# A recurrent scan of two directions with its per-head products laid on the two diagonal quarters of the matrix array, and with new ranks for its steps

## Chip, cores and metric

One core of one Trainium2 chip runs the whole program. The metric is the device time of one execution in microseconds (us). The kernel before takes 3224.84 us, the median of 3 runs (3218.99 to 3229.81).

## What is computed

The program is one block of a network on 1024 tokens of width 1024 and 256 context tokens. A projection feeds three parts: windowed attention (8 heads of 64), a recurrent scan (8 heads of 64) that runs over the tokens in both directions, and gates. Their results are merged, and a layer of 16 experts follows. The change concerns the scan. For each head it keeps a 64x64 state S and does, at each token:

```python
sa = jnp.einsum('bhvk,bhk->bhv', S, -kk_t)
S = (S * w_t[:, :, None, :] + sa[..., None] * (kk_t * a_t)[:, :, None, :]
     + v_t[..., None] * k_t[:, :, None, :])
y = jnp.einsum('bhvk,bhk->bhv', S, r_t) if emit else None
```

Each direction first goes over the 256 context tokens, of which no y is kept, and then over the 1024 tokens.

## The kernel before, in words

The tokens go in chunks of 64, so a direction has 20 steps: 4 for the context and 16 main ones. What a chunk needs is made ahead of the scan, in the feature stage (`feat`, one call for each of four column tiles `ct` of 128 features, that is, of two heads): the matrices X (from kk and r), AQ and BT (products within a chunk, masked or transposed) and WT (the inverse of a triangular 64x64 matrix, made on VectorE by `inv` and `inv_off`). They are written to DRAM (XD, AQD, BTD, WD; the values to vD), and each step of the scan loads its chunk from there.

The feature stage's inner loop, `jb` over 5 blocks of 4 chunks, runs 40 times in all (4 tiles, 2 directions). In each pass it makes X, copies AQ out of PSUM (L427), masks it (L429), writes it with three small DMAs (L430, L432; L433 in the context's block), transposes BK, copies BT out of PSUM on ScalarE (L440, a single buffer) and writes it to BTD with one DMA (L441). All these DMAs are issued by SP.

The scan is `rwkv_chain`, 20 steps for each of two directions, the directions in turn. A step of the kernel before does this:

- It loads its matrices with six or seven DMAs on SP (L527 to L534). AQ and UV hold two things one above the other: partitions 0 to 63 are for U (zeroed by GpSimd at L529 where it is not yet known), partitions 64 to 127 hold the values V.
- L538: X times the state S, four products with 128 rows, 128 columns and 128 moving columns. S holds the two heads of a tile as a block diagonal, half of it zeros.
- L541: AQ times UV for the eight heads, added to the same PSUM tile RY; 128 rows, 64 output columns, always the same output half (partitions 0 to 63).
- L545 and L546: RY is copied to R, negated; the even heads by ScalarE, the odd ones by VectorE to the upper partitions.
- L550: WT times R, eight products of 64x64x64, the even head on partitions 0 to 63 and the odd one on 64 to 127, in rows and in output.
- L553: the result U is copied into UV, the even heads by VectorE and the odd ones by ScalarE.
- L556: BT times UV, 128 rows, the output half alternating with the head.
- L561 and L562: the state gets the sum added and is scaled by the decay; VectorE, two instructions each, one for each half.
- In a main step, L565: AQ's second half times UV, all on output partitions 64 to 127; L568 copies y out of PSUM and L569 stores it, from ScalarE's queue.

A planner orders each engine's instructions when the program is built: it simulates the run and, of the instructions that are ready, takes the one with the lowest rank. A rank is the place in the order of the program; `low_priority(tc, n)` adds n to the ranks inside it. At run time each engine goes through its list in that order. The scan stands in the program ahead of the last seven of 16 gate projections (`proj` with `on_gate`, L258 and L265), ahead of the attention of tiles 0 and 1 (`att((0,1),...)`), the readout and the attention of tiles 2 and 3. Attention's tiles first load and rotate q and k (L627 to L643), then go through eight blocks each (`block`, L588 to L617). The scan's PSUM tiles, two for each direction, and those of attention 0 and 1 fill the eight banks; the readout and attention 2 and 3 take their banks over.

## Time and profile before

| | |
|---|---|
| median of 3 runs | 3224.84 us (3218.99 to 3229.81) |
| the profiled execution's own time | 3227.2 us |
| its span | 3225.4 us |
| TensorE (PE) busy | 2975.9 us, 92% |
| VectorE (DVE) busy | 2361.4 us, 73% |
| ScalarE (ACT) busy | 1742.2 us, 54% |
| GpSimd (POOL) busy | 639.5 us, 20% |
| mean granted clock of TensorE | 0.953 |

Rows are read as follows. PE is the stream of matrix products and PEld that of their weight loads; SPq and ACTq are queues that issue DMAs. A group of instructions has its line, engine, operation, tiles (out<-in), shape and count, then busy time and mean duration, then the engine's idle time just before its members and what ended it. A 32-bit product counts as two instructions on PE, so eight products show as x16. Products overlap in the array, so the spacing of a run of them is read from its whole length less the length of one, divided by one less than their count.

### The profile page before, as it was taken

How to read it: one execution, taken by the hardware profiler on the slowest of the kernel's cores; microseconds unless marked ns; L12 is line 12 of the kernel's file. 1: busy time of each engine (PE TensorE's matmuls, PEld its weight loads, DVE VectorE, ACT ScalarE, POOL GpSimd, SP SyncE). 2: the span in 40 equal slices, each digit the busy share in tenths (PEclk: the TensorE clock that was granted, in tenths of full speed). 3: DMA queues.
4: the chain of work that ended last, by engine and by line, in shares of the span. 5: the costliest groups of instructions: out<-in, count | busy, mean ns of one | idle time of the engine just before them, and what ended most of it. 6: DMA issues, size and time to landing. Idle time of an engine off the chain costs nothing.

```text
span 3225.4 us, 47429 instructions
## 1 busy us (share of the span) xinstructions
PE 2975.9 (92%) x17900; PEld 2366.1 (73%) x17900; DVE 2361.4 (73%) x3207; ACT 1742.2 (54%) x2006; POOL 639.5 (20%) x511
## 2 busy tenths in 40 slices
PE   7999999997878978899879999999999999999995
PEld 4777776776667764477668888888888878888884
DVE  5245455544376769757788999888898888888887
ACT  5343343433234334322357777777777777777775
POOL 2233333333241227211000000111010111010004
PEclk8998999998889999899889999999999999999998
DMA  5245554555778766444589999999999999999985
GB/s 205 82 121 137 124 128 123 129 142 131 158 185 203 189 166 219 146 152 151 198 315 384 388 372 370 357 363 377 380 362 363 358 365 376 381 362 362 363 319 229
DMA packets 537641, 825.18 MB, mean 256 GB/s; under 512 B 206590, under 2 KB 335742, under 8 KB 537284
## 3 DMA queue, kind: packets, MB, share of 16 engines
q1 hardware_dynamic: 490876, 747.60, 67.5%
q10 hardware_dynamic: 41176, 55.01, 5.4%
q0 software_dynamic: 5360, 19.54, 2.3%
q8 instruction: 141, 2.31, 0.3%
q14 instruction: 88, 0.72, 0.1%
HBM read 732.49 MB, written 89.55 MB: 255 GB/s over the span
## 4 chain that ended last, share of the span: by engine, by line
PE 45%; DVE 8%; issue 4%; DMA 3%; ACT 2%; POOL 1%; ACTq 0%; POOLq 0%; DVEq 0%; SPq 0%
PE ph L1016 22%; PE ye L1031 14%; DVE lo L915 4%; PE po L752 3%; PE pA L709 2%; PE pt L1053 1%; DMA raw<-in_w_e_dram 1%; ACT hi L914 1%; DVE oh L856 0%; DVE dl L1055 0%; PE pl L828 0%; PE apt L606 0%; PE yp L613 0%; DVE s L599 0%; DMA wmod<-in_w_mod_dram 0%
## 5 line engine op out<-in xcount | busy, mean ns | idle before, releaser
L915 DVE TENSOR_TENSOR lo<-raw,hi 128x2048 fp32r<-128x2048 f32 (+1 forms) x560 | 1197.5, 2170 | 107.9 <-ACT hi L914 92.0
L914 ACT CAST hi<-raw 128x2048 fp32r<-128x2048 f32 (+1 forms) x560 | 1009.8, 1813 | 353.7 <-PE ph L1016 191.0
L1016 PE MATMUL ph<-lo,xh 128*128 128x512 f32 (+1 forms) x1536 | 456.7, 378 | 23.4 <-DVE lo L915 23.1
L1016 PE MATMUL ph<-hi,xh 128*128 128x512 f32 (+1 forms) x1536 | 448.9, 374 | 3.1 <-ACT xh L886 2.0
L1016 PE MATMUL ph<-hi,xl 128*128 128x512 f32 (+1 forms) x1536 | 448.2, 373 | 0.0
L1016 PEld LDWEIGHTS ph<-lo,xh 128*128 128x128 f32 x1536 | 267.6, 188 | 95.4 <-DVE lo L915 48.3
L1016 PEld LDWEIGHTS ph<-hi,xh 128*128 128x128 f32 x1536 | 271.5, 188 | 55.9 <-ACT xh L886 2.4
L1016 PEld LDWEIGHTS ph<-hi,xl 128*128 128x128 f32 x1536 | 270.8, 188 | 52.7
L258 PE MATMUL pp<-uh,whi 128*128 128x512 f32 (+1 forms) x832 | 266.2, 392 | 4.8 <-DVE th L334 3.1
L258 PE MATMUL pp<-ul,whi 128*128 128x512 f32 (+1 forms) x832 | 267.4, 392 | 0.0
L258 PE MATMUL pp<-uh,wlo 128*128 128x512 f32 (+1 forms) x832 | 261.8, 387 | 0.5 <-issue 0.3
L864 POOL DMA_INDIRECT gath<-table,idx x16 | 37.9, 2368 | 958.6 <-DVE oh L856 587.7
L1031 PE MATMUL ye<-lo,dh 128*128 128x512 f32 x704 | 222.5, 397 | 1.1 <-DVE lo L915 0.9
L1031 PE MATMUL ye<-hi,dh 128*128 128x512 f32 x704 | 219.7, 393 | 2.5 <-ACT hi L914 1.3
L1031 PE MATMUL ye<-hi,dl 128*128 128x512 f32 x704 | 218.9, 392 | 3.3 <-DVE dl L1055 3.3
L258 PEld LDWEIGHTS pp<-uh,whi 128*128 128x128 f32 x832 | 155.0, 195 | 42.2 <-issue 7.1
L258 PEld LDWEIGHTS pp<-uh,wlo 128*128 128x128 f32 x832 | 156.6, 196 | 38.2 <-issue 8.8
L258 PEld LDWEIGHTS pp<-ul,whi 128*128 128x128 f32 x832 | 156.3, 196 | 37.5 <-issue 10.0
L292 DVE TENSOR_TENSOR tmp<-AU,W 120x144 f32<-120x144 f32 (+24 forms) x248 | 93.0, 375 | 115.8 <-DMA WD<-AU 40.0
L1031 PEld LDWEIGHTS ye<-hi,dl 128*128 128x128 f32 x704 | 132.8, 189 | 32.1 <-DVE dl L1055 3.7
L207 POOL TENSOR_TENSOR wlo<-wraw,whi 128x512 fp32r<-128x512 f32 x86 | 113.6, 1341 | 211.4 <-ACT whi L206 141.0
L1031 PEld LDWEIGHTS ye<-hi,dh 128*128 128x128 f32 x704 | 131.1, 189 | 30.7 <-ACT hi L914 2.0
(334 smaller groups left out, 4488.8 us busy)
## 6 DMA issues: line engine op xcount, KB each, us to landing
raw<-in_w_e_dram SPq DMA_DIRECT2D x430, 1024.0 KB
raw<-in_w_e_dram SPq DMA_DIRECT2D x128, 768.0 KB
wraw<-in_w_in_dram SPq DMA_DIRECT2D x86, 256.0 KB
wmod<-in_w_mod_dram SPq DMA_DIRECT2D x48, 256.0 KB
BTD<-BT SPq DMA_DIRECT2D x40, 256.0 KB
cBT<-BTD SPq DMA_DIRECT2D x40, 256.0 KB
wmod<-in_w_mod_dram SPq DMA_DIRECT2D x16, 512.0 KB
XD<-X SPq DMA_DIRECT2D x32, 256.0 KB
```

Of the source, the lines that this page charges most:

```text
L207: nc.gpsimd.tensor_sub(l[:,ks],r,h[:,ks].bitcast(F32))
L258: nc.tensor.matmul(p,wt[:,k,:],ut[:,k,a:a+b],start=(k==0 and first),stop=(k==7 and last))
L292: nc.vector.tensor_tensor(v,AU[d][:,:,s,ts_][:,:,None,:].to_broadcast([120,2,nj,L]), W[d][:,:,js,s:s+1].to_broadcast([120,2,nj,L]),op=ALU. ...
L709: nc.tensor.matmul(pq[q],w[:,kk,:],y[:,kk,q*512:(q+1)*512],start=(kk==0 and first),stop=(kk==3 and last))
L752: nc.tensor.matmul(pq[q],a[:,r],w[:,q*512:(q+1)*512],start=(k==0 and first),stop=(k==7 and last))
L864: gi=nc.gpsimd.indirect_dma_start(out=g,out_offset=None,in_=table[:,:], in_offset=bass.IndirectOffsetOnAxis(ap=idx[:,:1],axis=0))
L914: nc.scalar.copy(hi[:,:2*w],r[:,:2*w])
L915: li=nc.vector.tensor_sub(lo[:,:2*w],r[:,:2*w],hi[:,:2*w].bitcast(F32))
L1016: nc.tensor.matmul(PH[m][j][:,:c.stop-c.start],x[:,k,:],y[:,c],start=(k==0 and a),stop=(k==7 and b))
L1031: nc.tensor.matmul(ye[j],l[:,k,:],rr[:,j*512:(j+1)*512],start=st and a,stop=sp and b)
L1053: for k in range(n): nc.tensor.transpose(pt[:,k,:],hd[:,(k0+k)*128:(k0+k+1)*128],ident)
```

## The change

The two heads of a column tile are split by parity: even heads on partitions 0 to 63, odd heads on 64 to 127, for every operand of the scan. Every product becomes 64x64x64 with its rows and its output in the same half (`mm`, eight for a call, the halves in turn; its first two carry the start flag and the rest are ordered behind them). U and V have tiles of their own, so that the combined products with 128 rows become two with 64 each. S loses its zeros. R, U and y are copied by one ScalarE instruction each, over 128 partitions and 256 elements, and the state is updated by two VectorE instructions in place of four. GpSimd's memsets go. In program order the products with V alone are put ahead of those that need R. A main step has 64 products in place of 36, a context step 40 in place of 28. The DRAM tensors get the parity layout: the feature stage writes AVD and AUD in place of AQD, and BTD with four DMAs in place of one; vD and yD get twice the DMAs. On the host, g_up, gn and w_pr are permuted to match. Each pair of steps k = 4j+n gets `low_priority(tc, 2920-96k)`.

```diff
@@ host_layout
+    by=lambda a: np.ascontiguousarray(a.reshape(a.shape[0],4,2,64).transpose(0,2,1,3).reshape(a.shape[0],512))
+    o["g_up"]=by(i["g_up"][0])
...
@@ mixer
+    AVD=[dp.tile([20,128,4,128],F32,name=f"AVD{d}") for d in range(2)]
+    AUD=[dp.tile([20,128,4,64],F32,name=f"AUD{d}") for d in range(2)]
+    BTD=[dp.tile([20,2,128,4,64],F32,name=f"BTD{d}") for d in range(2)]
...
@@ on_v
-                    nc.sync.dma_start(vD[t0*128:(t0+nt)*128,ct*128:(ct+1)*128].rearrange("(a p) f -> p a f",p=128),vt[:,:nt])
+                    for hh in range(2):
+                        nc.sync.dma_start(vD[t0*128:(t0+nt)*128,hh,ct].rearrange("(a p) f -> p a f",p=128),vt[:,:nt,hh*64:hh*64+64])
@@ feat
-                        if jb: nc.sync.dma_start(AQD[d][cs,64:128,2*ct:2*ct+2,:].rearrange("c p h f -> p c h f"),AQ[64:128])
                         for hh in range(2):
-                            if jb: nc.sync.dma_start(AQD[d][cs,0:64,2*ct+hh,64:128].rearrange("c p f -> p c f"),AQ[0:64,:,hh,64:128])
-                            else: nc.sync.dma_start(AQD[d][cs,64:128,2*ct+hh,:w].rearrange("c p f -> p c f"),AQ[64:128,:,hh,:w])
+                            nc.sync.dma_start(AVD[d][cs,hh*64:hh*64+64,ct,:w].rearrange("c p f -> p c f"),AQ[64:128,:,hh,:w])
+                            if jb: nc.sync.dma_start(AUD[d][cs,hh*64:hh*64+64,ct].rearrange("c p f -> p c f"),AQ[0:64,:,hh,64:128])
...
-                        nc.sync.dma_start(BTD[d][cs,:,ct,:].rearrange("c p f -> p c f"),BT)
+                        for j in range(2):
+                            for hh in range(2):
+                                nc.sync.dma_start(BTD[d][cs,j,hh*64:hh*64+64,ct].rearrange("c p f -> p c f"),BT[j*64:j*64+64,:,hh*64:hh*64+64])
@@ rwkv_chain (the lines taken out are those told above)
+    H=[slice(0,64),slice(64,128)]
+    def mm(o,l,r,first=None,stop=False):
+        for ct in range(4):
+            for hh,h in enumerate(H):
+                b=first is not None and len(first)<2
+                z=nc.tensor.matmul(o[h,ct],l[h,ct],r[h,ct],start=b,stop=stop,skip_group_check=True)
+                if b: first.append(z)
+                elif first: tc.add_manual_dep(z.ins,first[hh].ins.name,mybir.DependencyInfo(mybir.DependencyClass.NoSync,mybir.DependencyReason.DATA),reason="order")
...
+        nc.sync.dma_start(AV[:,:,:M],G["AVD"][d][cc][:,:,:M])
+        for h,hh in zip(H,range(2)): nc.sync.dma_start(V[h],vD[cc*64:(cc+1)*64,hh])
         nc.sync.dma_start(X[:,:,:M],G["XD"][d][:,:,cc,:M].rearrange("a p f -> p a f"))
+        for h,hh in zip(H,range(2)):
+            nc.sync.dma_start(WT[h],G["WD"][d][:,cc*2+hh,0:64,:].rearrange("a s t -> s a t"))
+        nc.sync.dma_start(BT,G["BTD"][d][cc].rearrange("j p a k -> p j a k"))
+        if main: nc.sync.dma_start(AU,G["AUD"][d][cc])
+        RU=pR.tile([128,2,4,64],F32,name=f"RU{d}"); YS=pR.tile([128,2,4,64],F32,name=f"YS{d}")
+        mm(RU[:,0],AV[:,:,0:64],V,[],first)
+        if not first: mm(RU[:,0],X[:,:,0:64],S[d],stop=True)
+        R=p.tile([128,4,64],F32,name=f"R{d}",bufs=1)
+        nc.scalar.activation(R,RU[:,0],AF.Copy,scale=-1.0)
+        f=[]
+        mm(YS[:,1],BT[:,1],V,f)
+        if main:
+            mm(YS[:,0],AV[:,:,64:128],V,f)
+            mm(YS[:,0],X[:,:,64:128],S[d])
+        mm(RU[:,1],WT,R,stop=True)
+        nc.scalar.copy(U,RU[:,1])
+        mm(YS[:,1],BT[:,0],U,stop=True)
+        if not first: nc.vector.tensor_add(S[d],S[d],YS[:,1])
+        nc.vector.tensor_tensor(S[d],YS[:,1] if first else S[d],DL[d][:,:,cc:cc+1].to_broadcast([128,4,64]),op=ALU.mult)
+        if main:
+            mm(YS[:,0],AU,U,stop=True)
+            Y=p.tile([128,4,64],F32,name="Y",bufs=2)
+            nc.scalar.copy(Y,YS[:,0])
+            for h,hh in zip(H,range(2)): nc.scalar.dma_start(yD[d][(cc-4)*64:(cc-3)*64,hh],Y[h])
     for j in range(5):
         for n in range(4):
-            for d in range(2): step(j,n,d)
+            with low_priority(tc,2920-96*(4*j+n)):
+                for d in range(2): step(j,n,d)
```

## Rows read from the trace of the kernel before

**Rows 1.** the page: busy time of the engines; 40 slices of PE

```profile
PE 2975.9 (92%) x17900; PEld 2366.1 (73%) x17900; DVE 2361.4 (73%) x3207; ACT 1742.2 (54%) x2006; POOL 639.5 (20%) x511
...
PE   7999999997878978899879999999999999999995
```

**Rows 2.** stretches: us; PE, PEld, DVE, ACT, POOL busy; clock, DMA, GB/s

```profile
150.00:800.00 650.00, 602.78 (x3913) 470.24 (x3912) 321.79 (x680) 246.68 (x413) 227.72 (x172) 0.94 0.51 128
...
887.00:960.00 73.00, 50.80 (x588) 43.61 (x586) 51.33 (x113) 23.52 (x54) 31.45 (x34) 0.84 0.71 182
960.00:1020.00 60.00, 58.40 (x829) 50.19 (x828) 40.16 (x117) 27.77 (x65) 8.88 (x18) 1.00 0.82 208
1020.00:1060.00 40.00, 27.48 (x308) 22.24 (x308) 30.33 (x62) 16.66 (x41) 14.40 (x17) 0.82 0.75 187
1060.00:1160.00 100.00, 96.72 (x1240) 81.37 (x1240) 70.76 (x193) 40.71 (x97) 17.59 (x30) 0.95 0.78 194
1160.00:1212.00 52.00, 34.19 (x449) 29.96 (x448) 31.73 (x64) 16.51 (x41) 17.37 (x17) 0.87 0.60 151
1212.00:1360.00 148.00, 127.62 (x696) 66.59 (x697) 123.82 (x276) 63.95 (x144) 80.75 (x61) 0.91 0.61 188
```

**Rows 3.** tile RY: ns min/median/max, first and last start in us

```profile
L541 PE MATMUL RY<-UV,cAQ x640: 219/222/370, 886.8 to 1206.6; 128*64 128x64 f32 x160
...
L565 PE MATMUL RY<-UV,cAQ x512: 219/222/368, 959.7 to 1211.7; 128*64 128x64 f32 x171
```

**Rows 4.** timeline at 1000 us, PE: start, duration, line, tiles, count

```profile
1000.22 0.69 PE L556 MATMUL US<-UV,cBT 128*64 128x64 f32 x16
...
1001.65 0.68 PE L550 MATMUL US<-R,cWT 64*64 64x64 f32 x16
...
1003.49 1.16 PE L538 MATMUL RY<-S,cX 128*128 128x128 f32 x8
...
1004.58 1.15 PE L541 MATMUL RY<-UV,cAQ 128*64 128x64 f32 x16
```

**Rows 5.** groups, 887 to 1212 us: busy, mean ns | idle before, releasers

```profile
L538 PE MATMUL RY<-S,cX 128*128 128x128 f32 (+1 forms) x304 | 49.3, 313 | 23.1 <-issue 10.5 <-DVE S L562 5.8 <-ACT R L545 5.6
...
L565 PE MATMUL RY<-UV,cAQ 128*64 128x64 f32 x512 | 44.0, 233 | 1.4 <-DVE UV L553 1.3
L562 DVE TENSOR_TENSOR S<-S,DLs 64x256 f32<-64x256 f32 x74 | 42.7, 577 | 2.1
...
L550 PE MATMUL US<-R,cWT 64*64 64x64 f32 x640 | 37.0, 231 | 14.5 <-ACT R L545 7.3 <-DVE R L546 6.9 <-DMA UV<-vD 0.2
...
L561 DVE TENSOR_TENSOR S<-S,US 64x256 f32<-64x256 f32 x76 | 31.7, 418 | 20.2 <-PE US L556 18.8
L556 PE MATMUL US<-UV,cBT 128*64 128x64 f32 x640 | 30.3, 238 | 8.7 <-ACT UV L553 8.5
...
L568 ACT COPY Y<-RY 64x512 f32<-64x512 f32 x32 | 18.6, 582 | 40.3 <-PE RY L565 19.1 <-PE US L550 6.0 <-DMA cAQ<-AQD 5.2
...
L546 DVE TENSOR_SCALAR R<-RY 64x256 f32<-64x256 f32 x40 | 16.6, 418 | 33.3 <-ACT R L545 32.6
L553 DVE COPY UV<-US 64x256 f32<-64x256 f32 x40 | 16.5, 414 | 6.9 <-PE US L550 4.4 <-issue 1.1 <-POOL UV L529 0.8
...
L545 ACT ACTIVATE R<-RY 64x256 f32<-64x256 f32 x40 | 15.0, 377 | 57.2 <-PE RY L541 51.7 <-DMA vb<-vnD 3.7 <-PE US L556 1.5
L553 ACT COPY UV<-US 64x256 f32<-64x256 f32 x40 | 14.7, 369 | 56.7 <-DVE UV L553 50.4 <-DMA vb<-vnD 3.0 <-DVE m L592 2.5
```

**Rows 6.** tile BT, 150 to 820 us: its write; ACT waiting for it

```profile
L441 SPq DMA_DIRECT2D BTD<-BT x40: 359/565/1222, 175.4 to 814.9; - x40
...
  DMA BTD<-BT: 10.8, 7
```

**Rows 7.** waits, 1160 to 1212 us: us, times, longest

```profile
ACT KH L636 <- DMA qz<-kD: 6.4, 1, 6.4
```

**Rows 8.** tile yD: issue of a store on the ScalarE queue, ns

```profile
L569 ACTq DMA_DIRECT2D yD<-Y x32: 452/508/585, 963.7 to 1212.6; - x32
```

More of the change, by code (lines that the diff above doesn't have):

```diff
@@ L516, in rwkv_chain @@
     nc=tc.nc; vD=G["vD"]; yD=G["yD"]
-    S=[p.tile([128,4,2,64],F32,name=f"S{d}",bufs=1) for d in range(2)]
-    for d in range(2): nc.gpsimd.memset(S[d],0.0)
+    S=[p.tile([128,4,64],F32,name=f"S{d}",bufs=1) for d in range(2)]
     DL=[p.tile([128,4,20],F32,name=f"DLs{d}",bufs=1) for d in range(2)]
     for d in range(2): nc.sync.dma_start(DL[d],G["DLD"][d].rearrange("a p c -> p a c"))
+    H=[slice(0,64),slice(64,128)]
[6 more added lines that the diff above has]
+                elif first: tc.add_manual_dep(z.ins,first[hh].ins.name,mybir.DependencyInfo(mybir.DependencyClass.NoSync,mybir.DependencyReason.DATA),reason="order")
     def step(j,n,d):
@@ L530, in step @@
-        if main: nc.sync.dma_start(AQ[0:64,:,64:128],G["AQD"][d][cc][0:64,:,64:128])
-        nc.sync.dma_start(BT,G["BTD"][d][cc])
-        for hh in range(2):
-            nc.sync.dma_start(WT[hh*64:hh*64+64],G["WD"][d][:,cc*2+hh,0:64,:].rearrange("a s t -> s a t"))
-        nc.sync.dma_start(UV[64:128],vD[cc*64:(cc+1)*64,:])
-        RY=pR.tile([128,512],F32,name=f"RY{d}")
-        if not first:
-            for ct in range(4):
-                nc.tensor.matmul(RY[:M,ct*128:(ct+1)*128],X[:,ct,:M],S[d][:,ct].rearrange("p a b -> p (a b)"),
-                    start=(ct==0),stop=False,skip_group_check=True)
@@ L540, in step @@
-        for hd in range(8):
-            nc.tensor.matmul(RY[0:64,hd*64:(hd+1)*64],AQ[:,hd,0:64],UV[:,hd*64:(hd+1)*64],
-                start=(first and hd==0),stop=True,skip_group_check=True)
-        R=p.tile([128,4,64],F32,name=f"R{d}",bufs=2)
-        ry=RY[0:64].rearrange("p (a b f) -> p a b f",a=4,b=2)
-        nc.scalar.activation(R[0:64],ry[:,:,0,:],AF.Copy,scale=-1.0)
-        nc.vector.tensor_scalar_mul(R[64:128],ry[:,:,1,:],-1.0)
-        US=pR.tile([128,512],F32,name=f"US{d}")
-        for hd in range(8):
-            ct,hh=divmod(hd,2); h=slice(hh*64,hh*64+64)
-            nc.tensor.matmul(US[h,ct*64:(ct+1)*64],WT[h,ct,:],R[h,ct,:],start=True,stop=True)
@@ L551, in step @@
-        uv=UV[0:64].rearrange("p (a b f) -> p a b f",a=4,b=2); us=US[:,0:256].rearrange("p (a f) -> p a f",a=4)
-        for hh in range(2):
-            (nc.scalar.copy if hh else nc.vector.tensor_copy)(uv[:,:,hh,:],us[hh*64:hh*64+64])
-        for hd in range(8):
-            ct,hh=divmod(hd,2)
-            nc.tensor.matmul(US[hh*64:hh*64+64,256+ct*64:256+(ct+1)*64],BT[:,ct,hh*64:hh*64+64],
-                UV[:,hd*64:(hd+1)*64],start=True,stop=True)
-        sp=US[:,256:512].rearrange("p (a b) -> p a b",b=64)
@@ L559, in step @@
-        for hh in range(2):
-            h=slice(hh*64,hh*64+64); sd=S[d][h,:,hh,:]
-            if not first: nc.vector.tensor_add(sd,sd,sp[h])
-            nc.vector.tensor_tensor(sd,sp[h] if first else sd,DL[d][h,:,cc:cc+1].to_broadcast([64,4,64]),op=ALU.mult)
-        if main:
-            for hd in range(8):
-                nc.tensor.matmul(RY[64:128,hd*64:(hd+1)*64],AQ[:,hd,64:128],UV[:,hd*64:(hd+1)*64],
-                    start=False,stop=True,skip_group_check=True)
-            Y=p.tile([128,512],F32,name="Y",bufs=2)
-            nc.scalar.copy(Y[64:128],RY[64:128])
-            nc.scalar.dma_start(yD[d][(cc-4)*64:(cc-3)*64,:],Y[64:128])
+        X,AV=[p.tile([128,4,128],F32,name=f"{z}{d}") for z in ("cX","cAV")]
```

26 lines of the change are left out of this document (11 added, 15 removed).

## The prediction

> **What bounds the kernel now.** The busy line of the page comes first: PE is busy for 92% of the span and no other engine for more than 73% [rows 1]. PE's 40 slices then say where it isn't full; the experts' half, from slice 20 on, is at nines throughout, so what the scan can give back lies before it [rows 1]. The first and last starts of the tile RY place the scan: 886.8 to 1211.7 us [rows 3]. The stretches show PE there in two moods. From 960 to 1020 us and from 1060 to 1160 us it is full (58.4 of 60 us, 96.7 of 100): the scan's products and the blocks of attention lie side by side. From 887 to 960, 1020 to 1060 and 1160 to 1212 us it is idle for 22.2, 12.5 and 17.8 us [rows 2]. With the small rests of the full stretches that makes 57.4 us of 325. That is all that a scan with the same PE work can give back here. In the idle stretches the DVE is busier than the PE, or nearly so (51.3 of 73 us in the first), and the granted clock is 0.82 to 0.87 against 1.00 or 0.95 beside them [rows 2]. What comes after, 1212 to 1360 us, has the DVE at 123.8 of 148 us [rows 2]. It is the readout and the second half of attention; neither changes in amount, and neither can start before the scan's PSUM is free, so I let the gain of the scan carry through in full.
>
> What PE waits for within the scan is in the groups [rows 5]. Ahead of L538 it is idle for 23.1 us (state not ready, or issue), ahead of L550 for 14.5 (6.9 of it for R's second copy, on DVE), ahead of L556 for 8.5 (U's second copy, on ACT), ahead of L565 for 1.3. The copies in halves run one behind the other: DVE's R waits 32.6 us for ACT's R, ACT's U 50.4 us for DVE's U [rows 5].
>
> **The change part by part.** I make the sum against the profiled execution, 3227.2 us for a span of 3225.4; it lies 2.4 us above the median of the three runs.
>
> *PE work.* The spacing of a run of products is its length less one product's, over the count less one [rows 4], with the durations of [rows 3, 5]. L550, rows and outputs on alternating halves: (0.68-0.23)/15 = 0.030 us an instruction. L556, outputs alternating: 0.030. L541, always the same output half: (1.15-0.22)/15 = 0.062. L538: (1.16-0.31)/7 = 0.12. A main step before is 8x0.12 + 16x0.06 + 16x0.03 + 16x0.03 + 16x0.06 = 3.84 us; after, 8 calls of 16 instructions at 0.03 are 3.84 us too. A context step goes from 2.88 us (without L565) to 5x0.48 = 2.40. So the packing halves the cost of a product and the count doubles: 8 context steps x 0.48 = 4 us less, nothing on the main steps. The nearest row for the new form is L550, which has exactly its shape.
>
> The Trainium skill speaks against this: "TensorEngine Tiling (Array Packing)", section "Gotcha 1: PSUM Pressure", says that different row tiles cannot access the same PSUM bank at the same time, and the new products alternate row tiles within one bank. By that rule they would follow one another, and the sum would be that of the fourth rival below. The trace has the case already: L550's sixteen go through one bank on alternating row tiles at 0.030 us, half of L541's spacing [rows 4], so I keep the sum by the row.
>
> *Hand-overs.* A step's path from state to state was L538 and L541, R on ACT, R on DVE, L550, U on DVE, U on ACT, L556, and four DVE instructions. After, it is eight products, R (ACT), eight products, U (ACT), eight products and two DVE instructions; the products with V stand beside it. PE's waits for the second copies go: 6.9 + 8.5 + 1.3 = 16.7 us [rows 5]. Of the 23.1 us ahead of L538 I take half, as two of the four state instructions go: 11.5. That makes 28 us. Bounds: nothing, if the wait for ACT (7.3 us ahead of L550) grows by what goes; all idle time ahead of the four groups, 23.1+14.5+8.7+1.4 = 47.7 us. What is late next is ACT's copy.
>
> *DVE.* The scan's share was 42.7+31.7+16.6+16.5 = 107.5 us [rows 5]; after, 40 x (0.42+0.58) = 40, since time goes with the 256 elements and not with the partitions (ACT's and DVE's 64x256 forms are the only ones here; I take the 128x256 ones as equal). So 67 us less, by share of length 165/325, or 34 us, in the three idle stretches. PE is idle for 52.5 of those 165 us, so I count a third: 11 us. Bounds: nothing and 34, and with the hand-overs no more than the 57.4 us of idle.
>
> *ACT.* R, U and y took 15.0+14.7+18.6 = 48.3 us; after, 40 x (0.38+0.37) + 32 x 0.38 = 42. A main step issues two stores in place of one from ACT's queue, 32 x 0.51 = 16 us more [rows 8]. ACT is busy for 125 of 325 us [rows 2], so I take nothing. If half of the net 10 us falls into the idle stretches it is 5 us.
>
> *Loads of the scan and POOL.* SP issues seven loads in place of six in a context step and eight in place of seven in a main step, about half a microsecond each, 20 us more over 325. A second buffer of each operand hides them: a pair of steps takes 16 us. I take nothing. The memsets that go were on POOL, which is 20% busy [rows 1]: nothing.
>
> *Writes of the feature stage.* Here the change costs. A pass issues 11 DMAs in place of seven (nine for six in the context's block), all on SP, ahead of the next pass's writes and of the projections' weight loads. BT has one buffer, and its write is now four DMAs. At 0.565 us an issue the last is issued 1.7 us later. ACT already waited 10.8 us, in 7 of 40 passes, for that write [rows 6]. I let those seven grow by 1.7 us, 12 us, and hide a little behind PE's projections (PE 602.8 of 650 us busy [rows 2]): 10 us. Bounds: nothing, and all of it, 40 x 1.7 = 68 us. The twelve vD stores become 24, hidden among the rest. After the last pass nothing covers: the loads for the last inverse queue behind its writes, some 2 us, within the 10.
>
> *Ranks.* A main pair has 2 x 79 instructions, a context pair 102 (84 for the first): 2918 in all. So the first pair, 2920 ranks back, stands at the head of the gates, and each further pair is ranked 96 less far back; the last begins 938 ranks past the gates' head. The seven gates have some 400 instructions, so the later half of the scan ranks among attention's first blocks, where it had stood ahead of all. The gates were over when the scan began, because its inverse was not ready, so their part of the ranks moves little. Should the scan end last and alone, it isn't lost time: two directions need 2 x 3.84 = 7.7 us of PE for a pair, and a chain of three groups (0.7 us each with the last product's length), R, U and two DVE instructions is 3 x 0.7 + 0.38 + 0.37 + 0.42 + 0.58 = 3.9 us, so PE stays full. I take nothing; bounds: the 17.8 us of the last idle stretch as a gain (counted already), as much as a loss.
>
> Sum: -4 -28 -11 +10 = -33 us: 3227 - 33 = 3194 us.
>
> **The rivals.**
> 1. *The idle time goes altogether.* With V's products free to go anywhere and later steps ranked under attention, every gap finds work: 57.4 + 4 us, the writes hidden: 3166 us. For it: the two full stretches show that scan and attention together do fill PE. Against: the rotation of q and k, which the scan can't fill, waits for its own loads (6.4 us once [rows 7]).
> 2. *ACT takes the place of DVE as the wait.* All three copies of a step are now on ACT, whose list holds attention's instructions that wait for DMAs; a copy behind such a one stands still, as it did for 6.4 us behind KH's [rows 7]. Then the hand-overs give nothing, DVE 6 us, context 4, and the writes cost 10: 3227 us, no change.
> 3. *Slower: the single BT buffer.* Each pass waits for the fourth write, 68 us, against a gain of 43: 3252 us. It decides once more than 1.1 of the 1.7 us reach PE in every pass. For it: the buffer was already late in 7 passes. Against: the other 33 had slack, and the planner can put other ACT work ahead of the copy.
> 4. *The halves don't overlap.* At 0.06 us an instruction a main step costs 3.84 us more, a context step 2.40 less the 0.48 saved: 32 x 3.84 + 8 x 1.92 = 138 us more than now, in full stretches; with hand-overs, DVE and writes as above 3336 us. It is what the Trainium skill's rule gives. Against it stands L550's row.
>
> **How the numbers follow.** The forecast has 0.53, the rivals 0.14, 0.18, 0.11 and 0.04. A measurement of this kernel can tell some 0.3%, 10 us, from no change. The forecast's own range, with hand-overs and DVE from 14 to 57 us together and the writes from nothing to 25, is 3227-4-57 = 3166 to 3227-4-14+25 = 3234. To hold 8 in 10 I go to 3155 below, for part of the first rival with the scan and a better-placed readout, and to 3240 above, which takes in the second and the light end of the third. Faster: 0.50 of the forecast, the 0.14, 0.05 of the second: 0.69. Same: 0.03, 0.10 and 0.01 of the third: 0.14. Slower: 0.03 of the second, 0.10, 0.04: 0.17.
>
> **What would show it.** Right: runs of 16 products in about 0.7 us; a scan some 40 us shorter from first to last product; PE idle in its stretch at 20 us or less; no wait of PE for a second copy; ACT's wait for BT's write at 15 to 30 us, and the scan's start at 890 to 900 us. Wrong: sixteen products in 1.2 us (rival 4); the scan's start 40 us later or more (rival 3); PE waiting for ACT's R and U by as much as for both halves before (rival 2).

## The result: 82 us slower, and the profile after

The changed kernel takes 3307.74 us (median of 4 runs, 3306.51 to 3309.31), the kernel before on the same chip 3225.3: the ratio is 1.0257, 95% interval 1.0239 to 1.0275. The forecast was 3194 us, its range ended at 3240. The profiled execution took 3306.5 us for a span of 3304.7, against 3225.4 before: 79.3 us between the spans.

The page of the kernel after, its busy line and PE's 40 slices:

```profile
PE 3018.4 (91%) x19868; PEld 2393.2 (72%) x19868; DVE 2283.8 (69%) x3049; ACT 1733.3 (52%) x2006; POOL 593.8 (18%) x429
...
PE   7999999997778987799969999999999999999996
```

PE is busy for 42 us more than before [rows 1] and idle for 37 us more. To find where, take the tile `ph` at the head of the experts: its first product there starts at 1597.7 us before and at 1676.8 after, 79.1 us later, and from it to the end both kernels need the same time (1627.7 and 1627.9 us). So the whole loss lies ahead of the experts. Two views place it. First the tile `ph`, before and after:

```profile
L925 PE MATMUL ph<-lo,sc x16: 592/592/1057, 1597.7 to 1606.4; 128*2 128x512 f32 x16
...
L928 PE MATMUL ph<-lo,sc x16: 592/592/1057, 1676.8 to 1685.6; 128*2 128x512 f32 x16
```

Then the products of the scan in the kernel after, from the tiles RU and YS (ns min/median/max, first and last start in us); they answer to [rows 3]:

```profile
L535 PE MATMUL RU<-cV,cAV x640: 218/218/367, 892.3 to 1221.0; 64*64 64x64 f32 x160
...
L535 PE MATMUL YS<-U,cAU x512: 218/218/367, 964.5 to 1235.5; 64*64 64x64 f32 x171
```

The scan ends at 1235.7 us, 23.8 later than before (1211.9): it starts 5.5 us later and lasts 343.4 us in place of 325.1. From its end to the experts' first product it is 441.1 us in place of 385.8, 55.3 more. 23.8 + 55.3 = 79.1. The second term has its reason in the tile yh, which each block of attention writes once, 32 in all. Its writes up to the scan's end, before:

```profile
L616 ACT CAST yh<-yp x16: 245/266/267, 954.2 to 1186.1; 128x128 fp32r<-128x128 f32 x16
```

and after:

```profile
L618 ACT CAST yh<-yp x10: 266/266/267, 1002.9 to 1229.8; 128x128 fp32r<-128x128 f32 x10
```

Sixteen blocks, all of the first half of attention, lay beside the scan before; now ten do, and six stand behind it: if the 55.3 us are all theirs, 9.2 us each. The stretches of after (columns as in [rows 2]) show attention starving:

```profile
150.00:800.00 650.00, 604.74 (x3901) 468.94 (x3899) 321.75 (x675) 247.02 (x410) 225.62 (x172) 0.94 0.51 127
...
887.00:960.00 73.00, 54.19 (x787) 45.25 (x785) 25.30 (x42) 18.57 (x42) 23.61 (x19) 0.80 0.65 179
960.00:1020.00 60.00, 49.32 (x1171) 45.38 (x1172) 19.68 (x56) 14.90 (x38) 3.81 (x3) 0.88 0.66 186
...
1060.00:1160.00 100.00, 88.44 (x1447) 69.75 (x1443) 26.24 (x78) 25.03 (x66) 0.00 (x0) 0.90 0.61 165
...
892.00:1236.00 344.00, 281.62 (x5238) 235.85 (x5237) 116.67 (x300) 93.50 (x238) 40.19 (x32) 0.88 0.59 164
```

From 1060 to 1160 us DVE has 26.2 us of work where it had 70.8 [rows 2]; some 20 of these 45 us are the scan's own saving (67 over 325 us, by the prediction's estimate), the rest is attention that isn't there. PE, full there before, is idle for 11.6 of 100 us and has a lower clock. In the last row, the whole scan, PE is idle for 62.4 us, not fewer than the 57.4 of before.

What the scan waits for, 892 to 1236 us (groups, busy and mean ns | idle before, releasers), as in [rows 5]:

```profile
L535 PE MATMUL RU<-R,cWT 64*64 64x64 f32 x640 | 43.8, 244 | 14.8 <-ACT R L555 14.5 <-DMA cWT<-WD 0.2
...
L535 PE MATMUL YS<-cV,cBT 64*64 64x64 f32 x640 | 40.0, 243 | 8.3 <-ACT Y L569 5.9 <-DVE S L564 2.4
L535 PE MATMUL YS<-U,cBT 64*64 64x64 f32 x640 | 38.9, 243 | 10.1 <-ACT U L562 10.1
...
L535 PE MATMUL RU<-S,cX 64*64 64x64 f32 x608 | 35.3, 238 | 2.4 <-DVE S L565 2.4
...
L565 DVE TENSOR_TENSOR S<-S,DLs 128x256 f32<-128x256 f32 x38 | 19.1, 504 | 1.2
L564 DVE TENSOR_TENSOR S<-S,YS 128x256 f32<-128x256 f32 x38 | 15.9, 418 | 102.0 <-PE YS L535 101.8
L555 ACT ACTIVATE R<-RU 128x256 f32<-128x256 f32 x40 | 15.3, 382 | 63.6 <-PE RU L535 22.8 <-DMA yD<-Y 22.2 <-issue 7.1
```

PE's idle time ahead of X times S has fallen from 23.1 us to 2.4, but only 5.8 of the 23.1 was a wait for S [rows 5]; PE's waits for the state's two instructions are 8.3 us now (2.4 for L565, 5.9 for L564). DVE waits for PE, and PE waits for ACT's copies, while R on ACT waits 22.2 us at y's stores, which ACT's queue issues. They are the tile yD's, to be set beside [rows 8]:

```profile
L570 ACTq DMA_DIRECT2D yD<-Y x64: 452/554/1781, 966.1 to 1238.6; - x64
```

There are twice as many, and the longest takes three times as long.

### The profile page after: what moved, and what is told of

It is laid out like the page before. It is cut to its first block, busy times and chain, and to the rows that moved or that the text cites. A ratio compares the mean times of both kernels' runs of the same rounds, so it can differ in the third digit from the quotient of the medians.

```text
span 3304.7 us, 51301 instructions
## 1 busy us (share of the span) xinstructions
PE 3018.4 (91%) x19868; PEld 2393.2 (72%) x19868; DVE 2283.8 (69%) x3049; ACT 1733.3 (52%) x2006; POOL 593.8 (18%) x429
## 4 chain that ended last, share of the span: by engine, by line
PE 43%; DVE 9%; DMA 4%; issue 4%; ACT 3%; POOL 1%; ACTq 0%; POOLq 0%; DVEq 0%; SPq 0%
PE ph L1019 21%; PE ye L1034 13%; DVE lo L918 4%; PE pA L712 3%; PE po L755 2%; DMA raw<-in_w_e_dram 2%; PE pt L1056 1%; ACT hi L917 1%; PE yp L615 1%; PE apt L608 1%; DMA bt<-in_bias_dram 1%; DVE oh L859 0%; DVE dl L1058 0%; PE pl L831 0%; DVE KL L639 0%
```

## The experiments

Eighteen kernels. Three theories to begin with. **R**: the ranks put the later half of the scan behind work that waits for it. **P**: the small products cost PE more than their 0.03 us, by changes of shape or by the clock. **W**: the transfers of the feature stage. "Order" is the order of the products that the planner laid down on PE; it lays it down anew for each kernel. The times of all are in the table behind them.

**1. The change without its ranks.**

```diff
-            with low_priority(tc,2920-96*(4*j+n)):
-                for d in range(2): step(j,n,d)
+            for d in range(2): step(j,n,d)
```

> The changed kernel with the ranks of its scan steps taken away, so that the scan stands ahead of gates and attention as before; products, layout and writes are the changed ones. Theory R (the ranks cost the time: they let the planner put single attention instructions between single scan products, and hold the gates back behind the scan's products, so that attention starts late): 3200 to 3235 us, scan shorter than 300 us, few changes between scan and other products on PE. Rival P (the small products themselves cost it, by array mode changes and a lower clock): 3280 us or more. Rival W (the feature stage's writes cost it): 3290 us or more, as nothing there is undone.

3306.2 us, ratio 1.0256 (1.0227 to 1.0285): the time of the changed kernel. R's number falls; P's and W's lower bounds hold. The order is another one altogether, though: the scan runs alone, in 244.5 us, no block of attention stands beside it (10 of the 704 instructions of yp start by the scan's end, the first at 1134.9 us), and all 32 blocks follow. PE isn't full in such a scan, by this row (columns as in [rows 2]):

```profile
893.00:1138.00 245.00, 179.22 (x4778) 169.59 (x4777) 56.74 (x132) 55.76 (x140) 23.31 (x18) 0.90 0.74 205
```

Its waits from 892 to 1138 us (us in total, times, longest):

```profile
PE YS L535 <- ACT U L562: 56.3, 29, 4.1
...
ACT U L562 <- DMA yD<-Y: 60.2, 18, 4.7
```

So without the ranks, the new step keeps attention out (whether by its doubled list of products or by their place in the program isn't separated); the ranks bring ten blocks back in, and lengthen the scan by as much as these are worth.

**2. The ranks alone,** on the kernel before (the edit of 1, the other way round).

> The kernel before with the ranks alone (2920 less 96 for each pair of steps), old products, old layout, old writes. Theory R: slower than before by 30 to 80 us, 3255 to 3305. Rivals P and W: as before, 3225 us, within 10.

3248.97 us, 1.0069 (1.0043 to 1.0095): slower, by some 25 us, less than R's 30 to 80 and more than the 10 of the rivals. All 16 blocks stay beside the scan, which ends 21.3 us later. Ranks cost something by themselves.

**3. The writes alone:** BT's write in four, on the kernel before.

```diff
-    nc.sync.dma_start(BTD[d][cs,:,ct,:].rearrange("c p f -> p c f"),BT)
+    for j in range(2):
+        for hh in range(2):
+            nc.sync.dma_start(BTD[d][cs,j*64:j*64+64,ct,hh*64:hh*64+64].rearrange("c p f -> p c f"),BT[j*64:j*64+64,:,hh*64:hh*64+64])
```

> The kernel before with BT's one write per pass cut into the four that the change makes (halves by halves, runs of 256 bytes in place of 512), to the old layout; all else as before. Rival W: slower by 40 us or more. Theory R: what the changed kernel's feature stage shows, its last write 15 us later: 3230 to 3245 us; ScalarE's wait for the write at 40 to 60 us in place of 10.8.

3239.58 us, 1.0046 (1.0029 to 1.0064): some 15 us, R's number and not W's 40 or more, with the scan's start 7.7 us later.

**4. Later ranks.** The order of the kernel before was aimed at, by one constant.

```diff
-            with low_priority(tc,2920-96*(4*j+n)):
+            with low_priority(tc,4400-96*(4*j+n)):
```

> The kernel after, with the ranks of the scan's steps moved back by 1480 places (4400 in place of 2920) and nothing else: in the order laid down, the gates stand ahead of the scan again, and about as many of the attention's products stand ahead of the scan's end as in the kernel before (53 of some 100, after: 45), with some 170 changes between scan and other work on TensorE in place of 248. Theory O (the time was lost in the order: what the scan's stretch hid before, half of the attention, stands behind it now): most of the 82 us comes back, all but the 16 us of the feature stage's writes and some 10 us of ACT's queue: 3235 to 3260 us. Rival A (ACT's queue, which holds three copies and two store issues of every step): nothing is changed there, 3290 to 3310 us. Rival P (single small products among large ones: changes of shape on TensorE and a lower granted clock): a part comes back with the number of changes, 3265 to 3290 us.

3267.0 us, 1.0144 (1.0126 to 1.0161): half of the loss comes back, less than O expects; it is P's number. The 16 blocks are beside the scan again, but it ends 34.8 us later than before. Its waits, 893 to 1247 us:

```profile
ACT R L555 <- DMA yD<-Y: 51.2, 9, 7.8
...
PE RU L535 <- ACT R L555: 44.4, 13, 13.8
```

What stands in the way now, by these waits, is ACT's queue.

**5. U's copy and the stores off ACT,** in the changed kernel's own order.

```diff
-        nc.scalar.copy(U,RU[:,1])
+        nc.vector.tensor_copy(U,RU[:,1])
-            for h,hh in zip(H,range(2)): nc.scalar.dma_start(yD[d][(cc-4)*64:(cc-3)*64,hh],Y[h])
+            for h,hh in zip(H,range(2)): nc.gpsimd.dma_start(yD[d][(cc-4)*64:(cc-3)*64,hh],Y[h])
```

> The kernel after, with U copied by VectorE in place of ScalarE and y's two stores issued on GpSimd's queue in place of ScalarE's; the ranks stay. Rival A (ACT's queue is what the scan waits for): the waits of U behind the store issues go (38 us in this kernel's scan, 56 us in the kernel without ranks), the scan is 30 us shorter and the time 3265 to 3285 us. Theory O: the scan's own chain gets shorter but the order of the blocks stays as it is, so the time moves by less than 15 us, 3295 to 3310 us.

3299.53 us, 1.0231 (1.021 to 1.0252). The scan is 13.7 us shorter and ends 9.6 earlier; the same six blocks stand behind it. By itself ACT's queue is 8 us, within O's number.

**6. Two buffers for BT** (`bufs=1` to `bufs=2`).

> The kernel after, with two buffers for the tile BT in the feature stage in place of one, so that the copy into it does not wait for the four writes out of it. Theory W (ACT's wait of 60.6 us for these writes sets the scan's start 5 to 14 us late): the last write is issued some 10 us earlier, the scan starts 5 to 15 us earlier and the time falls by as much, 3290 to 3300 us. Theory O says the same of this part, since it took 16 us for it. If the writes cost by their number on the queues of SyncE, and not by the wait, nothing moves: 3305 to 3310 us.

3303.41 us, 1.0254 (1.0237 to 1.0272): nothing that a measurement can tell. What ACT waited for ahead of its copy into BT (us, times), in the kernel after:

```profile
  DMA BTD<-BT: 60.6, 23
```

and in this run:

```profile
  DMA BTD<-BT: 3.6, 1
```

ACT's wait goes from 60.6 to 3.6 us and the scan starts where it did (893.2 us). That wait was not on the path.

**7. All three edits** (4, 5, 6).

> The kernel after with the edits of the three runs before it together: ranks later, U on VectorE and the stores on GpSimd's queue, two buffers for BT. Theory O: the gains of the first and the third add up and the second counts some 10 us, now that the scan is what the attention's blocks stand among: 3215 to 3240 us, about the kernel before (3225). Rival A: the gains come from the second alone, 3255 to 3280 us. Below 3210 us the products on the diagonal would be worth something by themselves, once the order is mended.

3223.03 us, 0.9999 (0.9988 to 1.001): the time of the kernel before. One by one, the three had given 41, 8 and 4 us; together they give 85. Theory O is right in the size and wrong in that the second counts little.

**8. BT written whole,** on 7, and loaded in four parts by each step.

> The run with all three edits (ranks later, U on VectorE and the stores on GpSimd's queue, two buffers for BT: 3223 us), and the tile BT written whole again, in one transfer a pass, as the kernel before does; the scan's step then loads it in four parts in place of one (some 120 transfers go from the feature stage, as many come to the scan). Theory W' (the feature stage pays for the number of transfers that SyncE issues: 344 us of issue before, 447 after, between 150 and 900 us; the wait for BT's buffer was not it, since two buffers moved nothing): the scan starts 8 to 15 us earlier and the time is 3207 to 3216 us, below the kernel before. Rival (the transfers of the feature stage cost nothing once the order is mended, or the scan's loads cost as much): 3220 to 3228 us. Above 3235 us, the loads of the scan would be late.

3260.62 us, 1.012 (1.0103 to 1.0137). Both halves of the price are to be seen. The scan starts at 879.7 us, 22.3 earlier than in 7 and earlier than in the kernel before; but PE waits for the loads of its eleven transfers a step:

```profile
PE YS L533 <- DMA cBT<-BTD: 31.3, 14, 4.8
```

**9. As many blocks, more changes.** Ranks of 3600 in place of 4400: 298 changes between scan and other products in the order, in place of 168.

> The kernel after with the ranks moved back by 680 places (3600 in place of 2920): in the order laid down the gates stand ahead of the scan and 56 of the attention's products ahead of its end, as in the run with 4400 (53; 3267 us), but with 298 changes between scan and other work on TensorE in place of 168. Theory O (it is the work that the scan's stretch hides which counts): the same time as that run, 3260 to 3275 us. Rival P (the changes cost by their number, some 0.15 us each by the gaps between the products' starts in the kernel after): some 20 us more, 3280 to 3300 us.

3282.11 us, 1.0186 (1.0161 to 1.0212), 15 us over run 4: P's number. The two scans, first this run's, then run 4's (columns as in [rows 2]):

```profile
895.00:1266.00 371.00, 304.85 (x5364) 248.26 (x5363) 151.39 (x390) 115.76 (x295) 54.30 (x43) 0.85 0.58 161
```

```profile
893.00:1247.00 354.00, 280.83 (x5364) 238.36 (x5363) 149.13 (x390) 115.48 (x295) 55.12 (x44) 0.84 0.60 168
```

As many instructions, 5364, at about the same clock take PE 24.0 us more. Put down to 130 more changes that is an estimate of 0.18 us each.

**10. The stores alone** and **13. U's copy alone** off ACT, **18. both, with one buffer for BT**; all with the ranks of run 4.

> The kernel with the ranks moved back by 1480 places (3267 us), and only y's two stores moved from ScalarE's to GpSimd's queue; U stays on ScalarE, one buffer for BT. Theory A' (once the order is mended, the scan waits for ScalarE's queue, where the store issues stand: R waited 51 us for the store there, TensorE 44 us for R): most of the 44 us between that run and the one with all three edits comes back, 3225 to 3240 us. Rival 1 (it is ScalarE's three copies, not the stores): 3255 to 3270 us. Rival 2 (half and half): 3240 to 3255 us.

> The kernel with the ranks moved back by 1480 places (3267 us), and only the copy of U moved from ScalarE to VectorE; the stores stay on ScalarE's queue, one buffer for BT. With the stores alone moved it was 3254 us, with both and two buffers for BT 3223. If the two parts add up (and two buffers do nothing, as in the two runs that had them alone): 31 us less, 3230 to 3245 us. If each alone leaves the other as the wait, and only both together free the chain from R to U: 3250 to 3262 us.

> The run with all three edits (3223 us) with one buffer for BT, as in the kernel after: later ranks, U on VectorE and the stores on GpSimd's queue. With later ranks alone it was 3267 us, with the stores moved too 3254, with U moved too 3257. If only both together free ScalarE's queue and two buffers do nothing, as in the two runs that had them alone: 3221 to 3230 us. If the parts only add up, 13 and 10 us: 3240 to 3248 us, and the rest of the 44 us hangs on the two buffers, once the order is mended.

3254.0 us (ratio 1.0103, 1.0081 to 1.0124), 3257.02 (1.0088, 1.0057 to 1.012), and together 3225.76 (0.9997, 0.9986 to 1.0008). From run 4's 3267 the parts give 13 and 10 us, both give 41. With U alone moved, R still waits 54.6 us for the stores; with the stores alone moved, that wait is gone, and what U's copy still costs there shows in no wait. In run 18 R waits for PE:

```profile
ACT R L555 <- PE RU L535: 76.7, 16, 10.7
```

The second buffer has no part in it. How much of the 41 us is the queue isn't separated, since the order changed with it (below the table).

**11. Two buffers for BT on the kernel before,** and **16. its stores on GpSimd's queue,** as candidates for a faster kernel.

> The kernel before with two buffers for BT in place of one, to see whether it gains what the kernel after did not: ScalarE waited 10.8 us for that write in the kernel before. By the run with two buffers on the kernel after (no change that can be measured) 3220 to 3228 us. Rival: the waits were on the path in the kernel before, 3212 to 3218 us.

> The kernel before with y's one store a step issued on GpSimd's queue in place of ScalarE's, and nothing else: a candidate, since the stores cost the diagonal products 13 us. Before, ScalarE issued 31 of them, 16 us in the scan's 325. The laid-down order stays much as it was (52 of 99 of the attention's products ahead of the scan's end, 53 before; 176 changes, 166 before). Theory (16 blocks of the attention end with the scan, and then the first product of the experts comes 374 to 389 us behind the scan's end, as in all eleven kernels with 16 blocks so far): the scan's end tells the time; it comes up to 8 us earlier, 3216 to 3226 us. Rival (GpSimd's memsets of the next step stand behind the store, which waits for Y): the scan ends later, 3230 to 3250 us.

3226.1 us (1.0003, 0.9991 to 1.0014) and 3230.93 (1.0022, 1.0011 to 1.0033): no gain. In 16 the rival's time is right: the scan ends 8.3 us later. Its reason isn't shown. GpSimd waits for Y with each store, and the memset of an operand, in the same queue, 88.3 us for a step's products in place of 28.4 (waits, 886 to 1220 us), but all its waits ahead of that memset come to 158 us here and 163 before:

```profile
POOL cAQ L529 <- PE RY L565: 88.3, 13, 11.2
...
POOL yD L569 <- ACT Y L568: 22.3, 9, 8.7
```

**12. Fewer transfers,** on 7: BT written in two and loaded in two, WT loaded in one.

```diff
-    for j in range(2):
-        for hh in range(2):
-            nc.sync.dma_start(BTD[d][cs,j,hh*64:hh*64+64,ct].rearrange("c p f -> p c f"),BT[j*64:j*64+64,:,hh*64:hh*64+64])
+    for hh in range(2): nc.sync.dma_start(BTD[d][cs,:,hh,ct].rearrange("c p f -> p c f"),BT[:,:,hh*64:hh*64+64])
...
-        nc.sync.dma_start(BT,G["BTD"][d][cc].rearrange("j p a k -> p j a k"))
+            nc.sync.dma_start(BT[h],G["BTD"][d][cc][:,hh].rearrange("(j p) a k -> p j a k",j=2))
```

> The run with all three edits (3223 us) with BT in an order of its DRAM tile that needs two writes a pass in place of four (80 fewer in the feature stage) and two loads a step, while WT comes in one load in place of two: the loads of a step are eight as before. The run with BT written whole started its scan at 880 us, 22 us earlier than the run with all three, but its eleven loads a step were late (TensorE waited 31 us for BT). Theory W' (the number of transfers in the feature stage sets the scan's start, the number of loads a step sets its pace): the scan starts 8 to 18 us earlier than there, at 884 to 894 us, no wait for cBT grows, and the time is 3205 to 3215 us, below the kernel before. Rival (the scan's start is not what the end hangs on): 3218 to 3228 us.

3232.68 us, 1.0024 (1.001 to 1.0037). A miss of both: the scan starts at 882.1 us, 19.9 earlier than in 7, no load is late, and it ends 5.1 us later. From 890 to 960 us it has:

```profile
890.00:960.00 70.00, 50.14 (x644) 39.99 (x646) 42.16 (x101) 23.36 (x54) 16.55 (x13) 0.65 0.45 123
```

PE's granted clock is 0.65 there, a mean between its two levels of 1.2 and 2.4 GHz; it is 0.73 in run 7 and 0.83 in the kernel before. An earlier start wasn't worth its 20 us. Part of the reason is the order, which leaves more of the scan behind the last block than in 7 (below the table); why the clock is lower stays open.

**14. The scan alone, off ACT:** run 1 with the edit of run 5.

> The kernel after without its ranks (scan alone, 245 us for 40 steps; 3306 us) with U on VectorE and the stores on GpSimd's queue. There U waited 60 us for the store issues and TensorE 56 us for U. Theory (the scan alone is a chain of hand-overs, of which ScalarE's queue is a quarter, and no attention stands beside it, so that all it saves comes through): the scan takes 190 to 215 us and the time is 3255 to 3280 us. Rival (the loads that SyncE issues, about 5 us a step, set the pace of a scan alone: 211 us of issue in 245): the scan stays above 225 us and the time above 3285 us.

3312.13 us, 1.0261 (1.0232 to 1.029). The scan takes 211.6 us, 32.9 less, as the theory has it, and the time doesn't fall: the experts start 570.0 us after its end, in place of 537.9. The order has changed with the edit: the preparation of attention's first k (tile KL, 12 instructions), which ran beside the scan in run 1, from 908.2 to 918.7 us, stands at the scan's end here, from 1108.7 to 1118.5, and so do a gate's last products. So part of the saving went into work that moved. This run shows the case most clearly: a scan 114 us shorter than before, in a kernel 86 us slower.

**15. The kernel before with the ranks of run 4.**

> The kernel before with the ranks of the scan's steps at 4400 (the ranks of 2920 made it 25 us slower). If the ranks are harmful by what they put behind the scan (the gates, the first attention blocks), then with the gates ahead of the scan again and 50 of 95 of the attention's products ahead of its end it is within 10 us of the kernel before, 3218 to 3235 us. If alternating scan and attention by ranks costs by itself, whatever stands behind: 3240 to 3255 us.

3267.56 us, 1.0124 (1.0095 to 1.0152), 0.6 us from run 4, which has the new products in the same ranks. Both expectations were too low. The ranks cost 41 us by themselves, though 16 blocks stand beside the scan:

```profile
L617 ACT CAST yh<-yp x16: 243/266/268, 952.8 to 1141.4; 128x128 fp32r<-128x128 f32 x16
```

The last of them writes yh at 1141.4 us, 44.7 us earlier than before, and the scan goes on without them to 1257.7. From 1145 to 1258 us PE is busy for 84.5 of 113 us.

**17. Flatter ranks,** on 7 (3900 less 64 a step).

> The run with all three edits (3223 us) with ranks that fall more slowly (3900 less 64 a step, in place of 4400 less 96): in the laid-down order 55 of 102 of the attention's products stand ahead of the scan's end, with 198 changes in place of 192. Theory (what counts is where the scan and 16 blocks end together, and behind that 374 to 389 us to the first product of the experts): 16 blocks by the scan's end again, the scan's end between 1210 and 1235 us, the time 3213 to 3240 us, and equal to the scan's end plus 2005 to 2015 us within 10 us. Rival (the ranks' slope decides how many blocks stand behind the scan): fewer than 16 blocks by the scan's end, and 9 to 10 us more for each of them.

3232.86 us, 1.0029 (1.0017 to 1.0041): 16 blocks, the scan ends at 1210.7 us, the experts 387.1 later, all within the theory's bounds; scan's end plus 2022, 7 us past its figure but within the 10.

Medians, starts and ends in us; "blocks" are those that wrote yh by the scan's end, "tail" goes from the scan's end to the first product of ph at the head of the experts:

```
run                     time     scan              length  blocks  tail
before                  3225.3   886.8 to 1211.9   325.1   16      385.8
after                   3307.7   892.3 to 1235.7   343.4   10      441.1
1  no ranks             3306.2   892.8 to 1137.3   244.5    0      537.9
2  ranks alone          3249.0   888.9 to 1233.2   344.3   16      384.3
3  BT's writes alone    3239.6   894.5 to 1222.4   327.9   16      389.0
4  later ranks          3267.0   893.3 to 1246.7   353.4   16      388.2
5  off ACT              3299.5   896.4 to 1226.1   329.7   10      440.0
6  two buffers          3303.4   893.2 to 1237.1   343.9   10      437.0
7  4, 5 and 6           3223.0   902.0 to 1219.6   317.6   16      376.6
8  7, BT whole          3260.6   879.7 to 1251.7   372.0   16      376.6
9  most changes         3282.1   895.6 to 1265.8   370.2   16      385.5
10 4, stores            3254.0   895.8 to 1238.5   342.7   16      378.7
11 before, two buffers  3226.1   885.2 to 1211.8   326.6   16      386.1
12 7, fewer transfers   3232.7   882.1 to 1224.7   342.6   16      373.8
13 4, U                 3257.0   897.7 to 1244.1   346.5   16      383.4
14 1, off ACT           3312.1   897.5 to 1109.1   211.6    0      570.0
15 before, later ranks  3267.6   890.9 to 1257.7   366.8   16      381.1
16 before, stores       3230.9   886.6 to 1220.2   333.5   16      385.6
17 7, flatter ranks     3232.9   893.0 to 1210.7   317.7   16      387.1
18 4 and 5              3225.8   900.0 to 1214.3   314.3   16      377.1
```

The tail is 374 to 389 us with 16 blocks beside the scan, 437 to 441 with ten, 538 and 570 with none: against the kernel before 8.5 to 9.5 us for each block that is left, and 11.5 in run 14, where more than the blocks moved. The tails of runs 16 and 17 were forecast by that, and came out so; the time of 17 did too, that of 16 was the rival's. None of the eighteen is faster than the kernel before by more than a measurement can tell; 7, 11 and 18 equal it.

What the blocks leave out is how much of the scan stands behind the last of them. Counted in the traces from the last product of yp ahead of the scan's end, the scan's instructions on PE that follow it, and the us from there to the scan's last:

```
before                   248 of 2736    25.9
2  ranks alone           552 of 2736    53.4
15 before, later ranks  1288 of 2736   116.9
4  later ranks          2630 of 4704   125.8
10 4, stores            2626 of 4704   111.2
13 4, U                 2386 of 4704   117.6
18 4 and 5              2128 of 4704    92.4
7  4, 5 and 6           2138 of 4704    92.7
12 7, fewer transfers   2426 of 4704   105.1
after                     16 of 4704     1.2
```

That is where runs 2 and 15 lose their time: their last block is done earlier than before, and 28 and 91 us more of the scan follow it. It also shows that the edits on ACT's queue changed the order: at run 4's pace of 0.048 us an instruction, the 502 fewer of run 18 are worth an estimated 24 us of the 39 by which its scan is shorter.

## Why the prediction was wrong

**PE work: the price right, the sum not.** Seventeen of the new products in 0.68 us (after, PE from 1095 us; start, duration):

```profile
1095.20 0.68 PE L535 MATMUL YS<-cV,cBT 64*64 64x64 f32 x17
```

All of the scan's products together hold PE for 198.4 us (source L535 of after, the first row below). Before, RY holds it for 137.8 and US for 67.2 (the two others):

```profile
892.00:1236.00 344.00, 198.42 (x4704) 176.99 (x4704) 0.88 0.59 164
...
886.00:1212.00 326.00, 137.79 (x1456) 123.58 (x1456) 16.64 (x40) 33.05 (x72) 0.91 0.74 186
...
886.00:1212.00 326.00, 67.16 (x1280) 52.97 (x1280) 49.72 (x120) 14.72 (x40) 0.91 0.74 186
```

RY's and US's products overlap; with the overlap counted once they hold PE for 191.2 us in that trace. So the change costs 7 us here, where I had 4 less; in run 18 the products hold PE for 187.3 us, 4 less. Rival 4, by which the halves follow one another, would have made it some 330; what the Trainium skill, "TensorEngine Tiling (Array Packing)", section "Gotcha 1: PSUM Pressure", says of row tiles and one PSUM bank shows no price on these pairs of tiles, and the trace decides.

**Ranks: the step that failed.** I took nothing for them, within 17.8 us either way, on three grounds, and none holds. The gates' "part of the ranks moves little": the last gate's copy starts at 923.7 us in place of 893.2 (tile `gate`), and the first block of attention writes yh at 1002.9 in place of 954.2. What follows the scan "neither changes in amount", so that I "let the gain of the scan carry through in full": six blocks were added to it, and with them 55.3 us. And a scan that ends last and alone "isn't lost time", at 7.7 us of PE for a pair with PE full: in run 1, where it is alone, the 16 main pairs take 187.8 us (949.5 to 1137.3), 11.7 each, with PE busy for 139.0 of 187. The changed kernel's scan doesn't end alone; those of runs 2, 4 and 15 do.

Six blocks and 23.8 us of the scan are the whole 79 us. That the order leaves the blocks behind is shown by run 4: one constant, 16 blocks beside the scan, 41 us back. Runs 2 and 15, the ranks on the old products, show the other side: no block is lost, more of the scan stands alone, and 25 and 41 us go. Run 1 shows that leaving the ranks out is no cure: the new step in the planner's own order shuts attention out altogether. What the new products would be worth in the old order was not run; 7 and 18, the nearest, equal the kernel before.

**Hand-overs, -28: the bound of nothing came true.** The second copies' waits did go. Of the 23.1 us ahead of L538 I took half for the state, where only 5.8 waited for S; the waits for the state's instructions are 8.3 us after. And PE waited for ACT in place of the second copies: 14.5 + 10.1 + 5.9 us ahead of three groups, 30.5, where ACT's R and U before had cost it 7.3 + 5.6 + 8.5, 21.4 [rows 5]. That bound was named ("grows by what goes") and not believed; it was also the sign set down for rival 2. In the order of run 4 with ACT's queue freed the gain does show: scans of 318 and 314 us in runs 7 and 18, 8 and 11 us less than before.

**ACT, 0: mis-sized.** y's 64 stores take a median of 554 ns on ACT's queue, and R stands behind them. The stores and U's copy together are worth 8 us in the changed kernel (run 5) and 41 with later ranks (run 18 against run 4), the stores alone 13 there (run 10); part of the 41 is the order, by the estimate under the table. Rival 2 had the mechanism, ACT in DVE's place, at 3227 us, and too light: it left out the order.

**DVE, -11:** the amount was right, 19.1 + 15.9 us for the two state instructions where I had 40 with the first steps; but no gain shows: DVE was left idle (26.2 us of work from 1060 to 1160 us), as the attention that had needed it wasn't there.

**Writes, +10:** alone they cost 15 us (run 3), within the bounds. ACT's wait grew by 49.8 us to 60.6, in 23 passes, four times the 12 I allowed, and cost nothing that run 6 could show; so rival 3, the single buffer, falls too. What the number of transfers delays is the scan's start (22.3 and 19.9 us in runs 8 and 12); what that is worth at the end isn't settled, as run 12 lost it again.

**Loads of the scan, 0:** right for the eight of a step, as the groups show 0.2 us of wait for one (WT); eleven were too many (run 8).

**Context, POOL:** nothing speaks against them.

## What to carry to other kernels

A chain that other work fills is worth what the two take together: before counting what a shorter chain gives, count how many pieces of the filler still start before it ends, what one of them costs behind it (here some 9 us), and how much of the chain is left when the filler has run out. Instructions that halve in price and double in number are not neutral where a planner sets the order, and ranks that mend it must be tried with each list of instructions anew. And when two engines' copies move to one, look at what else that engine's queue issues; but where each edit has its own order, as here, remedies that give 13 and 10 us singly and 41 together don't tell queue from order.

## What the runs showed of the hardware

**A change of shape on TensorE has a price, and an equal shape none.** The kernel after, PE at 1093 us (start, duration, line, tiles, shape, count):

```profile
1093.50 0.33 PE L535 MATMUL RU<-S,cX 64*64 64x64 f32 x2
1093.76 0.33 PE L608 MATMUL apt<-ident,s 128*120 128x128 f32 x1
1094.01 0.32 PE L535 MATMUL RU<-S,cX 64*64 64x64 f32 x2
1094.27 0.32 PE L608 MATMUL apt<-ident,s 128*120 128x128 f32 x1
```

Two instructions of the scan and one transpose every 0.51 us, 0.25 from one start to the next at each change, where two instructions in a run of their own cost 0.06. In the kernel before, the scan's 128*64 products and attention's 120*64 ones went through each other with no pause:

```profile
1094.34 0.28 PE L613 MATMUL yp<-pT,vb 120*64 120x128 f32 x1
1094.35 0.33 PE L556 MATMUL US<-UV,cBT 128*64 128x64 f32 x2
1094.45 0.27 PE L613 MATMUL yp<-pT,vb 120*64 120x128 f32 x1
1094.56 0.57 PE L556 MATMUL US<-UV,cBT 128*64 128x64 f32 x13
```

The Trainium skill, "TensorEngine Tiling (Array Packing)", section "Key Properties", says that a change of the tiling mode drains TensorE, though not what it costs; these rows and the 0.18 us of run 9 agree with it. The new products have no shape in common with attention's blocks, the old ones had, and that was in no term of my sum. It is a small part of the 82 us, though: with rows and columns counted as 64 or 128, PE changes shape 271 times in the scan's stretch after and 256 times before, since the old products changed among their own shapes too.

**A queue that issues stores delays its engine's copies by more than the issue:** 0.52 us each by the median of run 4, but R waited 51.2 us in 9 places for them there, up to 7.8 us at a time. In that longest wait the four stores are issued only 4.8 us after y's copies, when an earlier store has landed, and R stands behind them.
